# Attention slots of a decoder trunk: short matmuls in one group, projections in one run, value weights' parts made partly earlier

## The chip, the cores and the metric

One core of a Trainium2 chip runs the whole program. Its engines work side by side, each through its own list of instructions in order: TensorE (PE in the profile, with its weight loads as PEld), VectorE (DVE), ScalarE (ACT), GpSimd (POOL) and SyncE (SP), which issues most transfers. The metric is the device time of one execution in microseconds (us). Lower is better.

## The reference

Two layers work on x of 1024 tokens by 1024 channels in float32. The first layer mixes tokens with a gated MLP on half of its columns and with eight heads of dilated attention on the other half, the second with gated linear attention; each is followed by a gated MLP with a causal convolution. The change lies in the first layer's mixer:

```python
def even_mixer(h, w_in, a_ln_g, a_ln_b, a_ws, a_bs, q_g, k_g, w_out):
    z = h @ w_in
    u, v, q, k, vb = jnp.split(z, [...], axis=-1)
    a_out = chunked_gmlp(gelu(u), gelu(v), a_ln_g, a_ln_b, a_ws, a_bs)
    qh, kh = rms_norm(heads(q), q_g), rms_norm(heads(k), k_g)
    vh = heads(vb)
    for window, dilation in ((128, 1), (512, 4), (2048, 16)):
        o_r, l_r = dilated_branch(qh, kh, vh, window, dilation)
        outs.append(o_r); lses.append(l_r)
    wts = softmax(stack(lses), axis=0)
    o = einsum('rbhs,rbhsc->bhsc', wts, stack(outs))
    return concatenate([a_out, b_out], axis=-1) @ w_out
```

`dilated_branch` attends within blocks of 128 tokens (the own block and the one before), after tokens have been gathered by the dilation. Heads have 64 channels.

## The kernel before

Numbers stay float32 in effect: an operand of a large product is split into a high part and the rest (`split`: a cast on ScalarE, a subtraction on VectorE), and a product is a sum over such parts.

`attention` (from line 870 of the profile's numbering) works in 64 slots. The eight heads form four pairs p; each pair has eight near units (the branch of dilation 1, one unit for each of eight blocks n) and then eight far units (the dilated branches together). `order` lists them. TensorE's work in a slot is of two sorts. The short matmuls belong to the attention itself:

- sc: the scores of a unit, two heads, 128 or 256 columns (`score`, line 885), followed by mask and minimum on VectorE and the exponential on ScalarE (both in tile sm)
- pP: the transposes of the exponentials (`turn`, line 911), copied to pT by ScalarE in odd units and by VectorE in even ones
- po: the outputs, pT times values (`output`, line 922), 4 or 8 matmuls of 64 columns
- tk: the transposes of keys (kd, by `ident`) and queries (qs, by `identr`) of a near unit (`Pair.turn`, line 992), read from one bank of PSUM (tag tq) by ScalarE and VectorE into kT and qT
- pm: the gating MLP's matmuls (`mix`, line 807), called out of the list `mixes`

The long matmuls come from the generator `work`: projections of queries, keys and values for the next pair (pj, 384 columns, 24 for a block of 128 tokens), and after the last pair the gating MLP's pv and pu (512 columns). `take(m)` issues the next m of them. A slot takes a share of 12 while a pair is left to be projected (13 in the first eight slots), and 21 after that. TensorE follows the order of these calls, since the matmuls are pinned to program order.

Before the change a slot issues: `parts` for the near unit three slots on (the normalised q and k are split or scaled, on POOL and VectorE), its own sc, half its share, the po of the slot before, tk for two slots on, the other half, and its pP. `weights()` stands once in each half and makes the split parts of one piece of weights for the next pair, out of the list `spread`, on ScalarE and VectorE; pieces with k under 4 are pinned to program order there. Three slots of preparation (the prologue) stand ahead of slot 0: `parts` of units 0 to 2, and from the second on 12 projections and one tk.

Weights' parts lie in pool wp (eight buffers) or, for some, in pool wx (four). Pair 2's first four pieces use wx, the rest of the pairs 1 to 3 uses wp. The value weights wv are split by `load_half` in one go, as soon as pair 3's projection reaches its fifth block and buffers come free.

Of the kernel before, what the change touches and what calls it, by code (L numbers as in the profile page):

```python
# [11 lines left out]
F32R = mybir.dt.float32r  # L12
U8 = mybir.dt.uint8
I32 = mybir.dt.int32
AF = mybir.ActivationFunctionType
# [5 lines left out]
P = 128  # L21
# [3 lines left out]
KD = D // P  # L25
# [3 lines left out]
PAIRS = 4  # L29
# [25 lines left out]
def f32(ap):  # L55
    return ap.bitcast(F32)
# [11 lines left out]
def trunk(ctx: ExitStack, tc: tile.TileContext, a, out):  # L68
    nc = tc.nc
    V, A, G, T, Q = nc.vector, nc.scalar, nc.gpsimd, nc.tensor, nc.sync  # L70
# [3 lines left out]
    wp = ctx.enter_context(tc.tile_pool(name="wp", bufs=NW, reuse_waits="tile"))  # L74
# [17 lines left out]
    g0 = small.tile([P, KD], F32, tag="g0", bufs=1, name="g0")  # L92
# [21 lines left out]
    def split(dst, src, hi=None, lo=None):  # L114

        (hi or A.copy)(dst[0], src)  # L116
        (lo or V.tensor_sub)(dst[1], src, f32(dst[0]))  # L117

    def turned(dst, t):

        raw = t.dtype == F32R
        return T.transpose(dst.bitcast(F32R) if raw else dst, t, identr if raw else ident)

    def scaled(dst, src, gain):

        split(dst, src, lambda o, x: A.activation(o, x, AF.Copy, scale=gain),
              lambda o, x, h: V.scalar_tensor_tensor(o, x, gain, h, op0=ALU.mult, op1=ALU.subtract))

    def load_raw(src, name, cols=D):
        raw = rawp.tile([P, D], F32, tag="raw", name=name)[:, :cols]  # L130
        Q.dma_start(raw, src)
        return raw

    def parts_of(src, name, pool=None, gain=None, **tag):

        w = (pool or wp).tile([P, 2, 512], F32R, **(tag or {"tag": "w"}), name=name)
        parts = [w[:, i, : src.shape[-1]] for i in range(2)]
        if gain is None:
            split(parts, src)
        else:  # L140
            scaled(parts, src, gain)
        return parts

    def load_w(src, name, width=512, n=2, gains=None):

        raw = load_raw(src, name + "r", n * width)
        return [parts_of(raw[:, i * width : i * width + width], f"{name}_{i}",
                         gain=None if gains is None else gains[:, i : i + 1]) for i in range(n)]

    def load_half(src, name, gains=None):  # L150

        return [w for kp in range(4)
                for w in load_w(src[kp], f"{name}{kp}", gains=None if gains is None else gains[:, 2 * kp : 2 * kp + 2])]
# [601 lines left out]
        V.scalar_tensor_tensor(mboth, count, -math.log(2.0), mboth, op0=ALU.mult, op1=ALU.add)  # L755
        yield

    def load_qkv(p, wx, between=None, spread=None):

        def part(k, src, gain):  # L760
            pin = tc.keep_in_program_order if k < 4 else lambda ins: ins
            if p == 2 and k < 4:
                w = wx.tile([P, 2, 384], F32R, tag="wx", name=f"wx{p}{k}")
            else:
                w = wp.tile([P, 2, 512], F32R, tag="w", name=f"wq{p}{k}")
            ws[k] = [w[:, i, : src.shape[-1]] for i in range(2)]
            split(ws[k], src, lambda o, x: pin(A.activation(o, x, AF.Copy, scale=gain)),
                  lambda o, x, h: pin(V.scalar_tensor_tensor(o, x, gain, h, op0=ALU.mult, op1=ALU.subtract)))

        ws = []  # L770
        for kp in range(4):
            raw = load_raw(a["w_qkv"][p, kp], f"wq{p}{kp}r", 768)
            if between:
                between(kp)
            for i in range(2):
                k = 2 * kp + i
                w = (2 * k) % 8 + k // 4 if p == 0 else k
                src, gain = raw[:, i * 384 : i * 384 + 384], g0[:, w : w + 1]
                if spread is not None:
                    ws.append(None)  # L780
                    spread.append(partial(part, k, src, gain))
                elif p % 2 or k >= 4:
                    ws.append(parts_of(src, f"wq{p}{kp}_{i}", gain=gain))
                else:
                    w = wx.tile([P, 2, 384], F32R, tag="wx", name=f"wx{p}{k}")
                    ws.append([w[:, j, :] for j in range(2)])
                    scaled(ws[-1], src, gain)
        return ws
# [49 lines left out]
    def pin(ins):  # L838
        return tc.keep_in_program_order(ins) if pinned else ins
# [31 lines left out]
    def attention(ps, at, av, pq, pq0, par0, wx, wq0, gqk, masks, rest, gm_open):  # L871
# [5 lines left out]
        def by4(t):  # L877

            return t.rearrange("p s (m r) -> p s r m", r=4)
# [51 lines left out]
        class Pair:  # L931
# [56 lines left out]
            def turn(self, n):  # L988
                qs, kd = self.qs[n]
                t = ps.tile([P, 4, P], F32, tag="tq", name=f"tk{self.p}{n}")  # L990
                for s in range(2):
                    pin(T.transpose(t[:, s, :], kd[:, s, :], ident))
                for j in range(2):
                    pin(turned(t[:, 2 + j, :], qs[:, j, :]))
                split([four(self.kT[:, i * 2 : i * 2 + 2], n) for i in range(2)], by4(t[:, :2]))
                qT = pq.tile([P, 2, P], F32R, tag="qT", bufs=3, name=f"qT{self.p}{n}")
                A.copy(qT, t[:, 2:])
                G.tensor_copy(four(self.qR, n), by4(f32(qT)))
                self.qT[n] = qT
# [54 lines left out]
        pairs, mixes, first, spread = [], [], [], []  # L1054
        slot = 0

        def weights():
            if slot and spread:
                spread.pop(0)()

        def soon(half, todo):
            mixes.extend([slot + 3 + k / 2, half, f] for k, f in enumerate(todo))

        def mix(when):
            while mixes and when(mixes[0]):
                mixes.pop(0)[2]()

        def work():
            ws = {0: wq0}
            for p in range(PAIRS):  # L1070
                def ahead():
                    ws[p + 1] = load_qkv(p + 1, wx, spread=spread) if p + 1 < PAIRS else load_half(a["w_vu"][0], "wv", g0)
                pairs.append(Pair(p, ws[p]))
                yield from pairs[p].project(ahead)
            par0.close()
            gm = gm_open()
            yield from gmlp(ps, gm, ws[PAIRS], soon)
            yield from u_proj(ps, gm, load_half(a["w_vu"][1], "wu", g0), lambda half: mix(lambda m: m[1] <= half), first)
# [3 lines left out]
        def take(m):  # L1082
            for _ in range(m):
                ins = next(stream, None)
                if ins is not None:
                    if pairs[0].done > 1:
                        tc.keep_in_program_order(ins)

        def need(p, n):
            while len(pairs) <= p or pairs[p].done <= n:  # L1090
                take(1)
# [12 lines left out]
        def turns(i):  # L1104
            p, kind, n = place_of(i)
            if kind == "n":
                pairs[p].turn(n)

        pinned.append(True)
        for i in range(3):  # L1110
            need(0, i + 2)
            parts(i)
            if i:
                take(12)
                turns(i - 1)
        need(0, BEGUN)
        previous = None
        for slot, (p, kind, n) in enumerate(order):
            share = RATE[0] if slot < NT else RATE[1] if len(pairs) < PAIRS or pairs[-1].done < NT else RATE[2]
            parts(slot + 3)  # L1120
            score, turn, output = pairs[p].near_unit(n) if kind == "n" else pairs[p].far_unit(n)
            score()
            weights()
            take(share // 2)
            if previous:
                previous()
            turns(slot + 2)
            mix(lambda m: m[0] <= slot)
            weights()
            take(share - share // 2)  # L1130
            mix(lambda m: m[0] <= slot + 0.5)
            turn()
            previous = output
            if kind == "n" and p and n in (4, 6):
                combine(pairs[p - 1], n // 2 - 2)()
        take(6)
        previous()
        for k, ins in enumerate(stream):
            pin(ins)
            if k % 12 == 11 and mixes:  # L1140
# [403 lines left out]
    def gm_open():  # L1544
        return gms.enter_context(tc.tile_pool(name="gm", bufs=1, side="right", reuse_waits="tile"))
# [13 lines left out]
    for l in range(2):  # L1559
        w_out = a["od_w_out" if l else "ev_w_out"]  # L1560
        x_in = (lambda n: x2[n]) if l else (lambda n: rows(a["x"], n))
        with ExitStack() as ops:
# [3 lines left out]
            pool = ops.enter_context(tc.tile_pool(name=f"op{l}", bufs=2, side="right", reuse_waits="tile"))  # L1566
# [41 lines left out]
        with ExitStack() as st:  # L1608
            pool = st.enter_context(tc.tile_pool(name=f"fd{l}", bufs=1, reuse_waits="tile"))
# [112 lines left out]
```

## Time and profile before

| | |
|---|---|
| median of 3 runs | 2118.29 us (2117.88 to 2118.57) |
| profiled execution | 2118.6 us |
| its span | 2116.9 us |
| granted clock of TensorE | 1.000 |
| TensorE busy | 2105.9 us, 99% |
| VectorE, ScalarE, POOL busy | 1536.3, 1055.7, 475.2 us |
| the attention stage | about 5.8 to 357 us of the span |

Times in rows of the timeline are from the span's start. A row gives start, duration, engine, line of the kernel, operation, tile written and tiles read, shapes and count; a bracket names the idle time ahead of it and what ended that. Tiles carry no numbers there: pT3n is any transposed tile of pair 3's near units. TensorE's matmuls are pipelined and their ends are modelled, so neighbouring rows overlap.

### The profile page before, as it was taken

The numbers are of one execution on the slowest core, as the hardware profiler recorded it, in microseconds if no ns is written. First come the engines' busy times: TensorE is split into PE (matmuls) and PEld (weight loads), VectorE is DVE, ScalarE is ACT, GpSimd is POOL, SyncE is SP. The second block draws the span as 40 slices with busy tenths as digits, with TensorE's granted clock in tenths as the row PEclk, the third lists the DMA queues.
The fourth block names the chain that finished last, engine by engine and source line by source line (L and its number), as shares of the span: only waits on it lengthen the run. The fifth ranks groups of instructions, "written<-read, shape, count | busy, mean of one in ns | idle before, by whom it ended". The sixth has DMA issues, their size and how long they took to land. (4 is left out here: it accounts for less than half of the span.)

```text
span 2116.9 us, 29739 instructions
## 1 busy us (share of the span) xinstructions
PE 2105.9 (99%) x10440; PEld 1794.1 (85%) x10440; DVE 1536.3 (73%) x2486; ACT 1055.7 (50%) x2061; POOL 475.2 (22%) x479
## 2 busy tenths in 40 slices
PE   8999999999999999999999999999999999999999
PEld 8999888888888888888899888888888888888887
DVE  7566564677879888655578777886788788785554
ACT  7556563365444444444454466745544444444443
POOL 5334310014325344000010011101224344220000
PEclk9999999999999999999999999999999999999999
DMA  7222314854444444765554243596544544458564
GB/s 250 59 75 65 101 50 156 306 199 157 165 144 159 169 164 150 263 229 203 207 191 156 87 137 134 169 328 239 196 162 155 169 164 154 155 179 299 204 227 160
DMA packets 170278, 367.08 MB, mean 173 GB/s; under 512 B 17632, under 2 KB 61408, under 8 KB 170128
## 3 DMA queue, kind: packets, MB, share of 16 engines
q1 hardware_dynamic: 169984, 365.05, 50.5%
q8 instruction: 82, 1.34, 0.3%
q14 instruction: 68, 0.56, 0.1%
q10 hardware_dynamic: 144, 0.13, 0.0%
HBM read 248.39 MB, written 115.93 MB: 172 GB/s over the span
## 5 line engine op out<-in xcount | busy, mean ns | idle before, releaser
L117 DVE TENSOR_TENSOR da<-ar,da 128x512 fp32r<-128x512 f32 x154 | 106.2, 690 | 155.1 <-ACT da L116 155.1
L116 ACT CAST da<-ar 128x512 fp32r<-128x512 f32 x154 | 96.0, 623 | 214.2 <-PE pdQ L427 101.6
L218 PE MATMUL po<-wo,hq 128*128 128x512 f32 x768 | 183.1, 394 | 0.0
L218 PEld LDWEIGHTS po<-wo,hq 128*128 128x128 f32 x768 | 142.1, 188 | 28.5 <-DVE hq L117 0.3
L218 PE MATMUL pv<-wv,hq 128*128 128x512 f32 (+2 forms) x768 | 142.2, 340 | 0.0
L427 PE MATMUL pdC<-dw,da 128*128 128x512 f32 x528 | 134.8, 390 | 0.0
L427 PE MATMUL pdB<-dw,da 128*128 128x512 f32 x528 | 134.8, 390 | 0.0
L218 PEld LDWEIGHTS pv<-wv,hq 128*128 128x128 f32 x768 | 118.7, 189 | 14.2
L218 PE MATMUL pj<-wq,hq 128*128 128x384 f32 x576 | 121.0, 343 | 0.0
L427 PEld LDWEIGHTS pdC<-dw,da 128*128 128x128 f32 x528 | 99.1, 188 | 20.5
L427 PEld LDWEIGHTS pdB<-dw,da 128*128 128x128 f32 x528 | 98.8, 188 | 20.3
L286 POOL TENSOR_TENSOR S1g<-rg 128x512 f32<-128x512 f32 x20 | 29.7, 1485 | 378.5 <-DMA wsd<-D 300.7
L117 DVE TENSOR_TENSOR dw<-wr,dw 128x512 fp32r<-128x512 f32 x154 | 105.6, 686 | 8.0 <-ACT dw L116 7.6
L161 POOL TENSOR_SCALAR rn<-ssq 128x1 f32<-128x1 f32 x22 | 9.1, 416 | 431.6 <-ACT h L181 242.5
L427 PE MATMUL pdO<-dw,da 128*128 128x512 f32 x396 | 100.5, 389 | 0.0
L116 ACT CAST dw<-wr 128x512 fp32r<-128x512 f32 x154 | 95.0, 617 | 6.6 <-DMA wr<-in_w_dn 2.9
L218 PEld LDWEIGHTS pj<-wq,hq 128*128 128x128 f32 x576 | 97.0, 189 | 0.0
L427 PEld LDWEIGHTS pdO<-dw,da 128*128 128x128 f32 x396 | 74.3, 188 | 15.4
L351 DVE SCALAR_TENSOR_TENSOR t<-g,cw,t 128x1022 f32<-128x1022 f32 x44 | 74.8, 1700 | 0.1
L335 DVE TENSOR_TENSOR g<-g,s1g 128x512 f32<-128x512 f32 x22 | 16.3, 741 | 78.7 <-ACT s1g L334 78.7
L350 DVE SCALAR_TENSOR_TENSOR t<-g,cw,t 128x1023 f32<-128x1023 f32 x44 | 59.4, 1350 | 14.8 <-ACT t L349 14.8
L161 POOL TENSOR_SCALAR ro<-oss 128x1 f32<-128x1 f32 x32 | 9.4, 294 | 255.5 <-ACT og L1437 255.5
(1052 smaller groups left out, 5480.8 us busy)
## 6 DMA issues: line engine op xcount, KB each, us to landing
ar<-actd SPq DMA_DIRECT2D x70, 512.0 KB, 3.6
rd<-in_w_down SPq DMA_DIRECT2D x44, 512.0 KB, 3.7
wsd<-D SPq DMA_DIRECT2D x88, 256.0 KB, 2.4
rg<-in_w_gate SPq DMA_DIRECT2D x40, 512.0 KB, 3.6
ru<-in_w_up SPq DMA_DIRECT2D x40, 512.0 KB, 4.9
wr<-wsd SPq DMA_DIRECT2D x40, 512.0 KB, 4.3
actd<-t SPq DMA_DIRECT2D x66, 256.0 KB, 2.2
wr<-in_w_dn SPq DMA_DIRECT2D x30, 512.0 KB, 5.0
```

What stands on the lines that cost most here:

```text
L116: (hi or A.copy)(dst[0], src)
L117: (lo or V.tensor_sub)(dst[1], src, f32(dst[0]))
L161: eng.tensor_scalar(r, ssq, 1.0 / n, EPS, op0=ALU.mult, op1=ALU.add)
L218: yield T.matmul(o, L[i], R[jj][:, sl], start=(k == 0 and (ii, jj) == PASSES[0]), stop=(k == nk - 1 and (ii, jj) == PASSES[-1]))
L286: G.tensor_tensor(sums[name], x, y, op=op)
L335: V.tensor_add(C22, C22, s1)
L350: V.scalar_tensor_tensor(t[:, 1:], g[:, : S - 1], w(1), t[:, 1:], op0=ALU.mult, op1=ALU.add)
L351: V.scalar_tensor_tensor(t[:, 2:], g[:, : S - 2], w(0), t[:, 2:], op0=ALU.mult, op1=ALU.add)
L427: T.matmul(o, L[ii][:, t * P : t * P + P], R[jj], skip_group_check=more, start=start and not more and (ii, jj) == PASSES[0], stop=stop and ...
```

## The change

A slot now issues, in this order: the po of the unit two slots back, the pP of the unit one slot back, its own sc, tk for two slots on, any pm that is due, one piece of weights, half the share, another piece, and the rest of the share. The two halves follow each other without anything for TensorE between them, so all short matmuls of a slot form one group and its projections one run. Outputs come one slot later. In the prologue 6 projections instead of 12 precede a tk. After the last slot come an output, the last pP, 9 long matmuls and the last output. Pieces of the gating (`soon`) are due two slots later for the second half of the tokens, and one instead of half a slot apart.

The spread part of `load_qkv` becomes `load_spread`, and the value weights go through it too: their pieces are put on the list when pair 3's projection reaches its fifth block, and are made two to a slot. Pair 3's last four pieces now lie in wx, so four buffers of wp are free for wv's first four as soon as pair 2's pieces there have been used.

```diff
--- before.py
+++ after.py
@@ -755,17 +755,25 @@
         V.scalar_tensor_tensor(mboth, count, -math.log(2.0), mboth, op0=ALU.mult, op1=ALU.add)
         yield
 
-    def load_qkv(p, wx, between=None, spread=None):
-
-        def part(k, src, gain):
+    def load_spread(src, name, width, gains, spread, pool):
+
+        def part(k, raw):
             pin = tc.keep_in_program_order if k < 4 else lambda ins: ins
-            if p == 2 and k < 4:
-                w = wx.tile([P, 2, 384], F32R, tag="wx", name=f"wx{p}{k}")
-            else:
-                w = wp.tile([P, 2, 512], F32R, tag="w", name=f"wq{p}{k}")
-            ws[k] = [w[:, i, : src.shape[-1]] for i in range(2)]
-            split(ws[k], src, lambda o, x: pin(A.activation(o, x, AF.Copy, scale=gain)),
+            own = pool(k)
+            w = own.tile([P, 2, 384], F32R, tag="wx", name=f"{name}{k}") if own else \
+                wp.tile([P, 2, 512], F32R, tag="w", name=f"{name}{k}")
+            ws[k] = [w[:, i, :width] for i in range(2)]
+            gain = gains[:, k : k + 1]
+            split(ws[k], raw, lambda o, x: pin(A.activation(o, x, AF.Copy, scale=gain)),
                   lambda o, x, h: pin(V.scalar_tensor_tensor(o, x, gain, h, op0=ALU.mult, op1=ALU.subtract)))
+
+        ws = [None] * KD
+        for kp in range(4):
+            raw = load_raw(src[kp], f"{name}{kp}r", 2 * width)
+            spread += [partial(part, 2 * kp + i, raw[:, i * width : i * width + width]) for i in range(2)]
+        return ws
+
+    def load_qkv(p, wx, between=None):
 
         ws = []
         for kp in range(4):
@@ -776,10 +784,7 @@
                 k = 2 * kp + i
                 w = (2 * k) % 8 + k // 4 if p == 0 else k
                 src, gain = raw[:, i * 384 : i * 384 + 384], g0[:, w : w + 1]
-                if spread is not None:
-                    ws.append(None)
-                    spread.append(partial(part, k, src, gain))
-                elif p % 2 or k >= 4:
+                if k >= 4:
                     ws.append(parts_of(src, f"wq{p}{kp}_{i}", gain=gain))
                 else:
                     w = wx.tile([P, 2, 384], F32R, tag="wx", name=f"wx{p}{k}")
@@ -1054,12 +1059,15 @@
         pairs, mixes, first, spread = [], [], [], []
         slot = 0
 
+        def wx_of(p):
+            return lambda k: wx if (p, k // 4) in ((2, 0), (3, 1)) else None
+
         def weights():
             if slot and spread:
                 spread.pop(0)()
 
         def soon(half, todo):
-            mixes.extend([slot + 3 + k / 2, half, f] for k, f in enumerate(todo))
+            mixes.extend([slot + 3 + 2 * half + k, half, f] for k, f in enumerate(todo))
 
         def mix(when):
             while mixes and when(mixes[0]):
@@ -1069,7 +1077,8 @@
             ws = {0: wq0}
             for p in range(PAIRS):
                 def ahead():
-                    ws[p + 1] = load_qkv(p + 1, wx, spread=spread) if p + 1 < PAIRS else load_half(a["w_vu"][0], "wv", g0)
+                    ws[p + 1] = load_spread(a["w_qkv"][p + 1], f"wq{p + 1}", 384, g0, spread, wx_of(p + 1)) if p + 1 < PAIRS else \
+                        load_spread(a["w_vu"][0], "wv", 512, g0, spread, wx_of(PAIRS))
                 pairs.append(Pair(p, ws[p]))
                 yield from pairs[p].project(ahead)
             par0.close()
@@ -1111,30 +1120,32 @@
             need(0, i + 2)
             parts(i)
             if i:
-                take(12)
+                take(6)
                 turns(i - 1)
         need(0, BEGUN)
-        previous = None
+        ended, scored = [], []
         for slot, (p, kind, n) in enumerate(order):
             share = RATE[0] if slot < NT else RATE[1] if len(pairs) < PAIRS or pairs[-1].done < NT else RATE[2]
             parts(slot + 3)
             score, turn, output = pairs[p].near_unit(n) if kind == "n" else pairs[p].far_unit(n)
+            for f in ended:
+                f()
+            for f, _ in scored:
+                f()
             score()
-            weights()
-            take(share // 2)
-            if previous:
-                previous()
             turns(slot + 2)
             mix(lambda m: m[0] <= slot)
             weights()
+            take(share // 2)
+            weights()
             take(share - share // 2)
-            mix(lambda m: m[0] <= slot + 0.5)
-            turn()
-            previous = output
+            ended, scored = [f for _, f in scored], [(turn, output)]
             if kind == "n" and p and n in (4, 6):
                 combine(pairs[p - 1], n // 2 - 2)()
-        take(6)
-        previous()
+        ended[0]()
+        scored[0][0]()
+        take(9)
+        scored[0][1]()
         for k, ins in enumerate(stream):
             pin(ins)
             if k % 12 == 11 and mixes:
```

TensorE in a near slot of pair 0 (sc0n40 and sc0n41 are the scores of unit 4 for its two heads, tk06 the transposes of unit 6, pT0n3 and pT0n2 the transposed exponentials of units 3 and 2). Before:

```order
L885 MATMUL sc0n40_991<-kT0_454,qT04_889 128x256 x2
L885 MATMUL sc0n41_997<-kT0_454,qT04_889 128x256 x2
L218 MATMUL pj10_972<-wq11_823,hq10_92 128x384
L218 MATMUL pj10_972<-wq12_869,hq00_90 128x384 x3
L218 MATMUL pj10_972<-wq13_892,hq10_92 128x384 x2
L922 MATMUL po0n0_810<-vN02_564,pT0n3_983 128x64
L922 MATMUL po0n0_810<-vN03_609,pT0n3_983 128x64
L922 MATMUL po0n0_810<-vN02_564,pT0n3_983 128x64
L922 MATMUL po0n0_810<-vN03_609,pT0n3_983 128x64
L992 MATMUL tk06_1017<-ident_78,kd06_912 128x128 x2
L122 MATMUL tk06_1017<-identr_83,qs06_909 128x128 x2
```

After:

```order
L927 MATMUL po0n0_847<-vN01_524,pT0n2_912 128x64
L927 MATMUL po0n0_847<-vN02_564,pT0n2_912 128x64
L927 MATMUL po0n0_847<-vN01_524,pT0n2_912 128x64
L927 MATMUL po0n0_847<-vN02_564,pT0n2_912 128x64
L916 MATMUL pP0n3_983<-ident_78,sm0n30_917 128x128 x2
L916 MATMUL pP0n3_983<-ident_78,sm0n31_923 128x128 x2
L890 MATMUL sc0n40_991<-kT0_454,qT04_876 128x256 x2
L890 MATMUL sc0n41_997<-kT0_454,qT04_876 128x256 x2
L997 MATMUL tk06_1003<-ident_78,kd06_901 128x128 x2
L122 MATMUL tk06_1003<-identr_83,qs06_898 128x128 x2
L218 MATMUL pj10_968<-wq11_820,hq10_92 128x384
L218 MATMUL pj10_968<-wq12_879,hq00_90 128x384 x3
```

The outputs are now unit 2's instead of unit 3's and stand ahead of the scores, pP of unit 3 has joined them, tk06 stands right behind the scores, and the six projections that parted scores and outputs are gone from there.

ScalarE around the value weights (sm are exponentials, wv0_0 to wv3_1 before and wv0 to wv7 after the eight pieces' high parts). Before:

```order
L959 ACTIVATE qn36_3344<-pj36_3239,r0_89 128x256
L961 ACTIVATE vN36_3346<-pj36_3239,r0_89 128x128
L891 ACTIVATE sm3n11_3338,ot3n0_3273<-sm3n11_3338,ot3n0_3273 128x256
L126 ACTIVATE wv0_0_3023<-wv0r_3021,g0_88 128x512
L116 CAST kT3_2623<-tk33_3362 128x8x32
L126 ACTIVATE wv0_1_3026<-wv0r_3021,g0_88 128x512
L126 ACTIVATE wv1_0_3031<-wv1r_3029,g0_88 128x512
L913 COPY pT3n1_3383<-pP3n1_3378 128x512
L126 ACTIVATE wv1_1_3034<-wv1r_3029,g0_88 128x512
L997 CAST qT33_3369<-tk33_3362 128x256
L891 ACTIVATE sm3n20_3393,ot3n0_3273<-sm3n20_3393,ot3n0_3273 128x256
L126 ACTIVATE wv2_0_3039<-wv2r_3037,g0_88 128x512
```

After:

```order
L964 ACTIVATE qn36_3354<-pj36_3249,r0_89 128x256
L966 ACTIVATE vN36_3356<-pj36_3249,r0_89 128x128
L1002 CAST qT33_3348<-tk33_3341 128x256
L767 ACTIVATE wv4_3132<-wv2r_3025,g0_88 128x512
L767 ACTIVATE wv5_3178<-wv2r_3025,g0_88 128x512
L767 ACTIVATE wv6_3187<-wv3r_3027,g0_88 128x512
L918 COPY pT3n1_3388<-pP3n1_3383 128x512
L116 CAST kT3_2633<-tk34_3402 128x8x32
L896 ACTIVATE sm3n20_3393,ot3n0_3273<-sm3n20_3393,ot3n0_3273 128x256
L767 ACTIVATE wv7_3232<-wv3r_3027,g0_88 128x512
L896 ACTIVATE sm3n21_3399,ot3n0_3273<-sm3n21_3399,ot3n0_3273 128x256
L1002 CAST qT34_3409<-tk34_3402 128x256
```

Four of the eight pieces (wv0 to wv3) have left this stretch for an earlier one, and wv4 to wv6 stand in a row ahead of the copy of pT3n1, which before had three pieces ahead of it and five behind it.

TensorE in the prologue, at the transposes of unit 1. Before:

```order
L218 MATMUL pj05_685<-wx00_341,hq01_91 128x384 x3
L218 MATMUL pj05_685<-wx01_344,hq01_91 128x384 x3
L218 MATMUL pj05_685<-wx02_356,hq01_91 128x384 x3
L218 MATMUL pj05_685<-wx03_359,hq01_91 128x384 x3
L218 MATMUL pj05_685<-wq02_0_367,hq11_93 128x384
L992 MATMUL tk01_704<-ident_78,kd01_635 128x128 x2
L122 MATMUL tk01_704<-identr_83,qs01_632 128x128 x2
L218 MATMUL pj05_685<-wq02_0_367,hq11_93 128x384 x2
```

After:

```order
L218 MATMUL pj05_685<-wx00_341,hq01_91 128x384 x3
L218 MATMUL pj05_685<-wx01_344,hq01_91 128x384 x3
L218 MATMUL pj05_685<-wx02_356,hq01_91 128x384
L997 MATMUL tk01_698<-ident_78,kd01_635 128x128 x2
L122 MATMUL tk01_698<-identr_83,qs01_632 128x128 x2
L218 MATMUL pj05_685<-wx02_356,hq01_91 128x384 x2
L218 MATMUL pj05_685<-wx03_359,hq01_91 128x384 x3
```

tk01 now stands six projections earlier in block 5.

## The prediction, made before the changed kernel ran

> **What bounds the kernel now.** I read the page first, for the engine that is busiest.
>
> ```profile
> span 2116.9 us, 29739 instructions
> PE 2105.9 (99%) x10440; PEld 1794.1 (85%) x10440; DVE 1536.3 (73%) x2486; ACT 1055.7 (50%) x2061; POOL 475.2 (22%) x479
> ```
>
> TensorE (PE) is busy 2105.9 of 2116.9 us. It leaves 11.0 us in all, so only TensorE's own time or one of its few waits can be won. The change touches only the attention of the first layer, so the next view is the busy time by stretch of it (columns: stretch, its length, busy time and count of PE, PEld, DVE, ACT and POOL, the granted clock, DMA share, GB/s).
>
> ```profile
> 36.00:100.00 64.00, 63.43 (x452) 61.82 (x451) 38.27 (x125) 42.23 (x128) 26.40 (x45) 1.00 0.22 64
> 100.00:232.00 132.00, 131.96 (x958) 130.24 (x957) 82.40 (x270) 78.44 (x248) 56.47 (x93) 1.00 0.28 77
> 232.00:240.00 8.00, 7.17 (x51) 6.29 (x50) 8.00 (x20) 7.57 (x20) 3.15 (x4) 1.00 0.61 179
> 240.00:357.00 117.00, 117.00 (x614) 99.22 (x613) 67.29 (x176) 60.60 (x118) 19.13 (x27) 1.00 0.27 84
> ```
>
> The clock is 1.00 throughout. TensorE waits in two places only: 0.57 us just after 36, and 0.83 us at 232 to 240, where VectorE is busy 8.00 of 8.00 us and ScalarE 7.57. Everywhere else its time is the sum of its matmuls, and the change issues the same matmuls. So the question is what a matmul costs in another neighbourhood, and what becomes of two small waits.
>
> **Grouping.** A near slot before alternates: weights' transposes and scores (pP, sc), six projections (pj), outputs and key transposes (po, tk), six projections. The timeline of TensorE (start, duration, both in us):
>
> ```profile
> 110.51 0.60 PE L911 MATMUL pP1n<-ident,sm1n 128*128 128x128 f32 x4
> 110.86 0.72 PE L885 MATMUL sc1n<-kT,qT 128*128 128x256 f32 x4
> 111.42 0.69 PE L218 MATMUL pj<-wq,hq 128*128 128x384 f32 x3
> 111.95 0.70 PE L218 MATMUL pj<-wx,hq 128*128 128x384 f32 x3
> 112.48 1.00 PE L922 MATMUL po1n<-vN,pT1n 128*128 128x64 f32 x8
> 113.32 0.39 PE L992 MATMUL tk<-ident,kd 128*128 128x128 f32 x2
> ...
> 113.67 1.28 PE L218 MATMUL pj<-wx,hq 128*128 128x384 f32 x6
> 114.79 0.60 PE L911 MATMUL pP1n<-ident,sm1n 128*128 128x128 f32 x4
> ```
>
> Durations overlap, so I price a group by starts: from its first row to the next group's first row, less the long matmuls between. The long matmul's price comes from an undisturbed run, and the same stretch shows the transposes alone:
>
> ```profile
> 25.31 2.24 PE L218 MATMUL pj<-wx,hq 128*128 128x384 f32 x12
> 27.39 0.34 PE L218 MATMUL pj<-wq,hq 128*128 128x384 f32 x1
> 27.57 0.38 PE L992 MATMUL tk<-ident,kd 128*128 128x128 f32 x2
> ...
> 27.91 2.15 PE L218 MATMUL pj<-wq,hq 128*128 128x384 f32 x11
> 29.89 0.33 PE L218 MATMUL pj<-wx,hq 128*128 128x384 f32 x1
> ```
>
> Twelve pj take 27.39 − 25.31 = 2.08 us, 0.173 each. Then pP and sc cost 112.48 − 110.51 − 6 × 0.173 = 0.93 us, po x8 with tk costs 114.79 − 112.48 − 1.04 = 1.27, and tk alone costs 29.89 − 27.57 − 11 × 0.173 = 0.41. The outputs alone stand in the far slots:
>
> ```profile
> 271.61 1.00 PE L922 MATMUL po3n<-vN,pT3n 128*128 128x64 f32 x8
> 272.42 2.79 PE L218 MATMUL pv<-wv,hq 128*128 128x512 f32 x11
> 275.05 0.38 PE L911 MATMUL pP3d<-ident,sm3d 128*128 128x128 f32 x2
> ...
> 275.74 2.46 PE L218 MATMUL pv<-wv,hq 128*128 128x512 f32 x10
> 278.04 0.56 PE L922 MATMUL po3d<-v,pT3d 128*128 128x64 f32 x4
> 278.41 2.79 PE L218 MATMUL pv<-wv,hq 128*128 128x512 f32 x11
> 281.03 0.60 PE L911 MATMUL pP3d<-ident,sm3d 128*128 128x128 f32 x4
> ```
>
> A pv takes (278.04 − 275.74) / 10 = 0.230, so po x8 alone costs 275.05 − 271.61 − 2.53 = 0.91 us, and po x4 costs 281.03 − 278.04 − 2.53 = 0.46. Two things follow. Half the matmuls cost half the time, so a group has no fixed price for its switch from and to long ones. And po with tk costs 1.27 where the two apart cost 0.91 + 0.41 = 1.32: transposes behind outputs save 0.05 us.
>
> After the change one group holds po, pP, sc and, in near slots, tk. Two joints are new and stand nowhere in the trace: po then pP (64 slots, less the first ones without an output), and sc then tk (29 slots that have both an output and a transpose; three of the 32 transposes are in the prologue). The transposes in pP go by ident like the first half of tk, so po then pP is nearest to po then tk and I take −0.05; its other end is 0. For sc then tk I take tk at its price alone, which gives the old saving back: +0.05, with −0.05 beside it at the other end had tk kept its saving there and sc shared too. In near slots the two cancel; in the 32 others 32 × −0.05 = **−1.6 us**. The ends are −1.6 − 29 × 0.05 = −3.1, all joints saving, and 29 × 0.05 = +1.5, none saving and tk's old saving gone.
>
> On this the Trainium skill speaks against the change: "TensorE: Matmul & The Clock Gate", section "Step-by-step: what each phase is for", says that the next weight load is pulled ahead and runs while the current matmul streams. By that, a short matmul right behind a long one has its load hidden, and a merged group has half as many such places. The trace does not agree for these groups: 0.46 is half of 0.91, so no first load is free.
>
> **Value weights.** Before, eight ScalarE casts and eight VectorE subtractions for wv come at once; now four of the pairs are made before pair 3's last units, four behind them. The wait and its cause:
>
> ```profile
> 230.45 0.86 PE L911 MATMUL pP3n<-ident,sm3n 128*128 128x128 f32 x4
> ...
> 231.62 1.21 PE L218 MATMUL pj<-wq,hq 128*128 128x384 f32 x6
> 233.45 1.10 PE L922 MATMUL po3n<-vN,pT3n 128*128 128x64 f32 x8 [0.62 <-ACT pT3n L913]
> ...
> 236.79 0.69 PE L218 MATMUL pj<-wq,hq 128*128 128x384 f32 x3
> 237.31 0.86 PE L218 MATMUL pv<-wv,hq 128*128 128x512 f32 x3
> 238.38 1.10 PE L922 MATMUL po3n<-vN,pT3n 128*128 128x64 f32 x8 [0.21 <-DVE pT3n L913]
> 230.73 0.71 ACT L126 ACTIVATE wv<-wv0r,g 128x512 fp32r<-128x512 f32 x1
> ...
> 232.84 0.56 ACT L913 COPY pT3n<-pP3n 128x512 f32<-128x512 f32 x1
> ...
> 238.09 0.72 ACT L126 ACTIVATE wv<-wv3r,g 128x512 fp32r<-128x512 f32 x1
> ```
>
> The first of eight casts starts at 230.73, the last at 238.09, and the copy of the transposed weights (pT3n) queues among them. TensorE loses 233.45 − 231.62 − 1.06 (the same six pj before an unhindered po, 111.42 to 112.48) = 0.77; 238.38 − 236.79 − 3 × 0.173 − 3 × 0.230 = 0.38; and 0.86 − 0.60 = 0.26 in the first pP. That is 1.41 us. In the new order four casts (4 × 0.72 = 2.9 us) remain there, three in a row ahead of one pT copy, but the copy's outputs now come a whole slot later, 4.28 us (113.32 less 4.28 is where the tk before it starts). The exponentials behind those casts are what is late next: casts 2.9, copy 0.56 and two exponentials of about 0.5 nearly fill the 4.28 us, and I leave 0.15 us for that. The term is **−1.3 us**, from 0 (the exponentials take the place of the copies) to −1.4. The four parts made early go to stretches where ScalarE is busy 78.44 of 132 us and VectorE 82.40; the buffers they need are freed with pair 2's last projections. Loads of the raw weights keep their queue and order.
>
> The gating's pieces (mx and pm) start up to 3.5 slots later, the combination of a pair's two branches stands ahead of the next copies on VectorE, and the last pair's outputs come one slot later. The instructions are the same, and what hides them is the room on VectorE and ScalarE in 240 to 357 us, 67.29 and 60.60 busy of 117. I take 0 for these together and carry their upper end in the small waits below: if that cover is gone, a pm or a pT waits as po does now, 0.2 to 0.6 us once. POOL's splits of q and k (qs, kd) are issued one slot ahead of tk as before, and tk stands half a run, about 1.0 us, nearer to them; POOL is busy 56.47 of 132 us, so this is 0 as well.
>
> **Prologue.** Six projections instead of twelve precede each early tk, so tk for units 0 and 1 comes 1.04 us earlier, and tk for unit 2 right behind unit 0's scores. There is one bank for tk, and it is read late; the second line is a statistics pass that ScalarE does ahead of the next unit's exponentials, the third the wait that is there now.
>
> ```profile
> 31.75 0.38 ACT L997 CAST qT<-tk 128x256 fp32r<-128x256 f32 x1 [0.49 <-DVE kT L117]
> 37.86 1.04 ACT L671 ACTIVATE xq<-xq 128x1024 f32<-128x1024 f32 x1
> 44.93 1.10 PE L922 MATMUL po0n<-vN,pT0n 128*128 128x64 f32 x8 [0.48 <-ACT pT0n L913]
> ```
>
> The present waits for pT0n (0.57 us by the window, with what durations hide about 1.0) go, since outputs come a slot later. In their place I expect tk for unit 1 to wait about 0.65 us for the bank's last reader at 31.75 and the first pP about as long for the exponential behind the 1.04 us pass. The term is **0**, from −0.9 (nothing new) to +0.8 (both, with a second tk late).
>
> **Sum.** −1.6 − 1.3 + 0 = −2.9 us; I add +0.2 for small new waits (between 0 and 0.5, the size of the present ones), which gives −2.7. The profiled execution took 2118.6 us, 1.7 above its span and 0.3 above the median of 2118.29. So 2115.9 for such an execution, 2115.6 against the median. About 0.2% (4.24 us) is what a measurement of this kernel can tell from no change: the bounds are 2114.05 and 2122.53.
>
> **The rivals.** First, grouping buys nothing: the joints cost 0 on balance, and only the weights' term counts. 2118.29 − 1.3 = 2117.0. For it speaks that half a group costs half; against it, the 0.05 between po and tk.
>
> Second, everything gains: −3.1 − 1.4 − 0.9 = −5.4, 2112.9. It needs sc then tk to share as po then tk does, and a prologue without any new wait.
>
> Third, slower: the single tk bank. Its reads go ScalarE, VectorE, ScalarE, and weight parts queue among them:
>
> ```profile
> 109.42 1.61 DVE L768 SCALAR_TENSOR_TENSOR wq<-wq23r,g,wq 128x384 fp32r<-128x384 f32 x2
> 111.46 0.37 ACT L997 CAST qT<-tk 128x256 fp32r<-128x256 f32 x1 [1.38 <-DVE kT L117]
> ```
>
> The tk of 109.04 is read to the end at 111.83, 2.8 us on, since VectorE does 1.61 us of wq first. The next one comes at 4.28 us, so 1.5 us is left; the two parts per slot now stand elsewhere in the queues. If they delay each read by more than that, every excess 0.1 us costs 2.4 us over the 24 near slots of pairs 0 to 2. It decides from 0.3 us on: 24 × 0.3 = 7.2, less 2.7, gives 2122.8. Against it speaks the 1.5 us of room, nearly one whole slot's weight work.
>
> Fourth, slower too: the merged group loses one hidden weight load a slot. A po costs 0.91 / 8 = 0.11, so 61 joints × 0.11 = +6.7, with −1.3 for the weights 2123.7. The halves of po speak against it. The page named above stands behind this one; by that rule it would come so, by the trace not.
>
> **How the numbers follow.** My sum, with its terms between their ends, 0.44; grouping without effect 0.22; everything gains 0.20; the bank 0.07; the lost load 0.05; small waits that eat the gain, within 0.2%, 0.02. That makes faster 0.20, same 0.68, slower 0.12. I predict 2115.7 us. The range reaches from 2113.2, near the case where everything gains, to 2119.8, where no joint saves (+1.5) and the weights' wait stays: it leaves out both slow rivals and a little of the fast end.
>
> **What would show it.** In the timeline: near slots of 4.28 us or less; a far group of po x8, pP x2 and sc at 1.55 instead of 0.91 + 0.69 = 1.60 (0.69 is 278.04 − 275.05 − 2.30); TensorE's idle time at 230 to 240 under 0.3 us instead of 0.83; a wait of about 0.65 us before the second tk at 30 to 32. Wrong would be waits on qT, kT or the exponentials inside near slots, or near slots over 4.35 us.

## The result and the profile after

The changed kernel took 2114.57 us (median, 2114.19 to 2115.71), the kernel before, run beside it, 2118.36 us. The ratio is 0.9982, 95% interval 0.9975 to 0.9989: 3.8 us faster, between 2.3 and 5.3. The profiled execution took 2114.53 us with a span of 2112.8, against 2118.6 and 2116.9 before. Two more timings of the changed kernel, taken as a base for the experiments, gave 0.9985 and 0.9981. The median of before moved between 2118.3 and 2119.0 from chip to chip, so each kernel is compared by its ratio to before on the same chip.

The page, then the busy time of the same four stretches (stretch, length, busy time and count of PE, PEld, DVE, ACT, POOL, clock, DMA share, GB/s), then TensorE's waits in the attention:

```profile
span 2112.8 us, 29740 instructions
PE 2102.1 (99%) x10440; PEld 1793.6 (85%) x10440; DVE 1533.2 (73%) x2486; ACT 1058.7 (50%) x2063; POOL 471.3 (22%) x479
36.00:100.00 64.00, 63.58 (x459) 62.87 (x458) 38.52 (x123) 42.02 (x129) 26.56 (x46) 1.00 0.22 64
100.00:232.00 132.00, 131.95 (x966) 131.54 (x964) 84.39 (x281) 82.97 (x255) 56.41 (x91) 1.00 0.27 78
232.00:240.00 8.00, 8.00 (x58) 7.39 (x57) 6.39 (x18) 4.81 (x17) 4.88 (x8) 1.00 0.94 277
240.00:357.00 117.00, 117.00 (x616) 99.83 (x615) 62.85 (x166) 62.13 (x115) 14.87 (x23) 1.00 0.23 74
...
PE pP0n L916 <- ACT sm0n L896: 0.4, 1, 0.4
PE tk L997 <- ACT qT L1002: 0.3, 1, 0.3
```

TensorE is busy 3.8 us less with the same 10440 matmuls. That is not all matmuls that cost less: their ends are modelled, so short waits are hidden inside busy time, and the sums below separate the two. The stretch of the value weights has no idle time left, 8.00 of 8.00, with ScalarE down from 7.57 to 4.81. Two waits are still listed, both early: tk for the reader of its bank, and a pP for an exponential.

The timeline of TensorE after, one near slot and two far ones of pair 3, to be held against 110.51 to 114.79 and 271.61 to 281.03 before:

```profile
117.06 1.00 PE L927 MATMUL po1n<-vN,pT1n 128*128 128x64 f32 x8
117.90 0.61 PE L916 MATMUL pP1n<-ident,sm1n 128*128 128x128 f32 x4
118.26 0.72 PE L890 MATMUL sc1n<-kT,qT 128*128 128x256 f32 x4
118.82 0.38 PE L997 MATMUL tk<-ident,kd 128*128 128x128 f32 x2
...
119.16 2.34 PE L218 MATMUL pj<-wq,hq 128*128 128x384 f32 x12
121.34 1.00 PE L927 MATMUL po1n<-vN,pT1n 128*128 128x64 f32 x8
...
270.15 1.00 PE L927 MATMUL po3n<-vN,pT3n 128*128 128x64 f32 x8
...
276.49 0.56 PE L927 MATMUL po3d<-v,pT3d 128*128 128x64 f32 x4
...
282.57 1.00 PE L927 MATMUL po3d<-v,pT3d 128*128 128x64 f32 x8
```

A near slot takes 121.34 − 117.06 = 4.28 us, as before. Two far slots of pair 3 take 282.57 − 270.15 = 12.42 us. Before it was 12.63, by these two rows of the old trace:

```profile
271.61 1.00 PE L922 MATMUL po3n<-vN,pT3n 128*128 128x64 f32 x8
284.24 1.00 PE L922 MATMUL po3d<-v,pT3d 128*128 128x64 f32 x8
```

So a far slot among pv saves 0.10 us. Far slots among pj, before and after, with two slots between the rows:

```profile
133.14 1.00 PE L922 MATMUL po1n<-vN,pT1n 128*128 128x64 f32 x8
140.28 1.00 PE L922 MATMUL po1d<-v,pT1d 128*128 128x64 f32 x8
```

```profile
132.89 1.00 PE L927 MATMUL po1n<-vN,pT1n 128*128 128x64 f32 x8
139.89 1.00 PE L927 MATMUL po1d<-v,pT1d 128*128 128x64 f32 x8
```

7.14 us became 7.00, 0.07 a slot. Pairs 0 to 2 have 24 slots without tk and the last pair has ten. If each saves what these few do, 0.07 and 0.10, grouping gives 1.7 + 1.0 = 2.7 us, an estimate. The value weights' waits, 1.41 us by the prediction's rows, are gone. Idle time in the early waits went from 0.57 to 0.67 us (0.25 at the second tk, 0.42 between 36 and 100). Together −2.7 − 1.4 + 0.1 = −4.0, against 4.1 between the two spans and 3.8 between the medians.

The starts of single matmuls give a second account, in which waits that the modelled ends hide are seen too. From the 25th projection to the end of the stage the two traces differ by 4.2 us. About 1.9 of it stands at the joints of the groups (34 slots without tk at 0.05 each give 1.7), 0.8 inside the runs, and 1.5 in waits. The waits at the value weights, 1.65 us by this count, are gone. The early ones go from 1.5 to 1.3 us, and those of pP for exponentials in far slots grow from 0.2 to 0.6. Outside this stretch the two traces differ by −0.3 us ahead of it and by +0.4 behind it. No run shows the cause of these two.

### The profile page after: what moved, and what is told of

The parts are those of the page before. It is cut to its first block, busy times and chain, and to the rows that moved or that the text cites. A ratio compares the mean times of both kernels' runs of the same rounds, so it can differ in the third digit from the quotient of the medians.

```text
span 2112.8 us, 29740 instructions
## 1 busy us (share of the span) xinstructions
PE 2102.1 (99%) x10440; PEld 1793.6 (85%) x10440; DVE 1533.2 (73%) x2486; ACT 1058.7 (50%) x2063; POOL 471.3 (22%) x479
## 5 line engine op out<-in xcount | busy, mean ns | idle before, releaser
L218 PE MATMUL pj<-wq,hq 128*128 128x384 f32 x672 | 128.6, 339 | 0.0
L218 PEld LDWEIGHTS pj<-wq,hq 128*128 128x128 f32 x672 | 114.8, 188 | 0.0
```

What stands on the lines that cost most here:

```text
L218: yield T.matmul(o, L[i], R[jj][:, sl], start=(k == 0 and (ii, jj) == PASSES[0]), stop=(k == nk - 1 and (ii, jj) == PASSES[-1]))
```

## The experiments

Where the text gives a group's price to the nanosecond, it is counted from the starts of the single matmuls in the trace, from the last long one ahead of the group to the second one behind it, less the two long ones.

**The value weights alone** (slot order, prologue and gating of before):

```diff
-ws[p + 1] = load_qkv(p + 1, wx, spread=spread) if p + 1 < PAIRS else load_half(a["w_vu"][0], "wv", g0)
+ws[p + 1] = load_spread(..., spread, wx_of(p + 1)) if p + 1 < PAIRS else load_spread(..., spread, wx_of(PAIRS))
```

> The slot order and prologue of before, with only the value weights' part of the change: their pieces two to a slot, four of them ahead of pair 3's end, pair 3's last four pieces in the other pool. Theory A (fewer casts in one place remove the wait): the three TensorE waits at 230 to 240 us, 1.65 us together in the trace of before, go almost wholly, 2118.4 - 1.5 = 2116.9 us. Theory B (what removed them is that outputs come a slot later): at least one po of pair 3 still waits 0.3 to 0.8 us for its pT behind the remaining casts, and the time is 2117.4 to 2118.2 us. Groups and their prices stay as before in both.

Ratio 0.9994 (0.9986 to 1.0003), −1.3 us. The medians alone do not tell this from no change; the timeline does, in which one po still comes late:

```profile
231.07 1.22 PE L218 MATMUL pj<-wq,hq 128*128 128x384 f32 x6
232.32 1.10 PE L927 MATMUL po3n<-vN,pT3n 128*128 128x64 f32 x8
```

It starts 1.25 us after the run instead of 1.06, where before it was 1.83, and the other two waits are gone. Fewer casts in the place are enough for most of it. What is left goes with the outputs' old place half a slot behind pP: the changed kernel, which differs here in the slot's order, has no such wait.

**The grouping alone** (value weights split at once, pair 3's pieces in the old pool):

```diff
-load_spread(a["w_vu"][0], "wv", 512, g0, spread, wx_of(PAIRS))
+load_half(a["w_vu"][0], "wv", g0)
-... in ((2, 0), (3, 1)) else None
+... in ((2, 0),) else None
```

> The changed slot order and prologue, but the value weights split in one go as before and pair 3's pieces in the old pool. Theory A (grouping saves about 2.0 us at the joints and 0.8 us in the long runs, the waits for weights are another matter): some wait at the value weights comes back, now in pP for the exponentials, 0.5 to 1.6 us, and the time is 2115.0 to 2116.3 us. Theory B (later outputs hide the casts): no TensorE wait over 0.3 us there, and the time is that of the changed kernel, 2114.6 us.

Ratio 0.9988 (0.9980 to 0.9997), −2.5 us. The two halves of the change add up to the whole, −1.3 and −2.5 against −3.8, each known to about 1.8 us either way. A wait came back, but not where either theory had it:

```profile
233.71 0.72 PE L890 MATMUL sc3n<-kT,qT 128*128 128x256 f32 x4
235.42 0.41 PE L997 MATMUL tk<-ident,kd 128*128 128x128 f32 x2 [0.99 <-ACT qT L1002]
...
233.07 1.34 ACT L126 ACTIVATE wv<-wv2r,g 128x512 fp32r<-128x512 f32 x2
234.29 0.73 ACT L126 ACTIVATE wv<-wv3r,g 128x512 fp32r<-128x512 f32 x1
234.90 0.37 ACT L1002 CAST qT<-tk 128x256 fp32r<-128x256 f32 x1
```

The read of the one tk bank (qT) stands on ScalarE behind three casts of wv, and the next tk waits for it. Later outputs do take pT out of the way of the casts; the bank is then what is late.

**Scores last in the group, tk ahead of pP:**

```diff
 for f in ended: f()
+turns(slot + 2)
 for f, _ in scored: f()
 score()
-turns(slot + 2)
```

> The changed kernel with tk moved inside the group, from behind the scores to between outputs and pP. Theory C (a joint from outputs to transposes saves 0.04 to 0.05 us, and what the long run pays is set by the group's last short matmul: after tk or po it pays, after sc it does not): near groups of 2.172 us fall to about 2.12, 29 x 0.05 = -1.5 us, 2113.1 us. Theory D (each group saves one joint whatever stands last): near groups stay at 2.17 us and the time at 2114.6 us. A loss would be pP waiting longer for nothing here, since tk stands ahead of it, or sc for its kT.

Ratio 0.9992 (0.9983 to 1.0001). The near slots did get cheaper:

```profile
113.43 1.00 PE L927 MATMUL po1n<-vN,pT1n 128*128 128x64 f32 x8
114.27 0.39 PE L997 MATMUL tk<-ident,kd 128*128 128x128 f32 x2
...
117.64 1.00 PE L927 MATMUL po1n<-vN,pT1n 128*128 128x64 f32 x8
```

4.21 us instead of 4.28; the group costs 2.119 instead of 2.172, the 0.05 expected. The kernel is slower than the changed one all the same, by 2.1 us, so waits took this back and more:

```profile
PE tk L997 <- POOL kd L988: 0.6, 1, 0.6
PE tk L997 <- issue: 0.5, 1, 0.5
PE tk L997 <- ACT qT L1002: 0.5, 1, 0.5
```

**Outputs apart again**, alone between the two halves of the run:

```diff
-for f in ended: f()
 for f, _ in scored: f()
 score(); turns(slot + 2); mix(...); weights(); take(share // 2)
+for f in ended: f()
 weights(); take(share - share // 2)
```

> The changed kernel with the outputs taken out of the group and put between the two halves of the run, alone there. Theory C (the joint from outputs to pP is what saves): every slot loses it, 61 x 0.05 = +3.0 us, and the six matmuls behind each break run some ns slower, +0.8, so 2118.4 us. Theory D (only the number of runs counts, the joint itself saves nothing): +0.8 us at most, 2115.4 us.

Ratio 1.0008 (0.9999 to 1.0017), 5.5 us over the changed kernel's 0.9982, and no better than before though the value weights' part is in it. Near slots:

```profile
112.86 1.00 PE L927 MATMUL po1n<-vN,pT1n 128*128 128x64 f32 x8
...
117.18 1.00 PE L927 MATMUL po1n<-vN,pT1n 128*128 128x64 f32 x8
```

4.32 us. By single starts the group of pP, sc and tk costs 1.332 and po alone 0.895, 2.227 together against 2.172 in one group; in far slots 0.701 + 0.895 = 1.596 against 1.543. So the joint from outputs to pP is worth 0.05 us a slot. The joints are not the whole of the loss. By single starts the trace loses 4.7 us in the stage against the changed kernel's: about 2.8 at the joints, 1.1 inside the runs, and 0.9 in waits, which neither theory had. At the joints merging is not a gain by itself; what follows the outputs is.

**A prologue of 12 projections** (`take(12)` for `take(6)`):

> The changed kernel with 12 projections instead of 6 ahead of each early tk. Theory A (the second tk waits for the last reader of the one tk bank because it comes 1.04 us earlier): that wait of 0.45 us falls to 0.15 us or less, but the waits of pP for exponentials in the first units stay: 0.1 to 0.4 us faster than the changed kernel. Theory B (the wait only moves, because slot 0 comes at the same place): no difference over 0.1 us, the wait standing at a later tk or pP.

Ratio 0.9987, against 0.9985 for the changed kernel timed beside it: no difference. The wait moved one tk on:

```profile
31.73 0.38 PE L997 MATMUL tk<-ident,kd 128*128 128x128 f32 x2
...
35.86 0.41 PE L997 MATMUL tk<-ident,kd 128*128 128x128 f32 x2 [1.06 <-ACT qT L1002]
```

The changed kernel itself, as base of this and the next two:

> The changed kernel itself, on the same chip as the next three, as their base: 3.8 us under before, as in its first runs. The waits in its prologue (0.45, 0.27 and 0.58 us) may differ a little with the arrival of the first weights.

**tk apart**, between the halves:

```diff
 score()
-turns(slot + 2)
 mix(...); weights(); take(share // 2)
+turns(slot + 2)
 weights(); take(share - share // 2)
```

> The changed kernel with tk taken out of the group and put between the two halves of the run. Theory C (the price of a group is set by what stands last in it): the group's rest then ends on sc at 1.76 us and tk alone costs 0.41, together the 2.17 us of now, so near slots lose nothing at the joints and only the run's matmuls behind each break run slower, +0.3 to +0.5 us in all. Theory D (each further break costs one joint of 0.05 us): 29 x 0.05 = +1.5 us more, +1.9 us in all.

Ratio 0.9991 (0.9982 to 1.0000) against 0.9985; the difference lies within the intervals. The groups are unambiguous: 1.759 without tk and 0.414 for tk alone, 2.173 against 2.172. Breaking the run costs nothing at the joint from scores to tk. In its trace three tk lost 0.24, 0.24 and 0.56 us to waits.

**tk and scores exchanged:**

```diff
 for f, _ in scored: f()
-score()
 turns(slot + 2)
+score()
```

> The changed kernel with tk and sc exchanged: outputs, pP, tk, scores. tk stands 0.55 us earlier than in the changed kernel and 0.35 us later than in the run with tk ahead of pP, where it waited 1.6 us in all for kd and the bank. Theory C: near groups with scores last cost 2.12 us instead of 2.17, 29 x 0.05 = -1.5 us; if tk's waits stay under 0.3 us in all, 1.2 to 1.5 us faster than the changed kernel. Theory E (the 0.55 us eats the room of kd and of the bank): waits of 0.5 to 1.5 us at tk come, and the time is that of the changed kernel within 0.5 us.

Ratio 0.9994 (0.9985 to 1.0003). The group costs 2.176 us: nothing won, though the scores stand last. That refutes the form in which I had put the rule. The starts show where the price goes. The first wide matmul behind tk holds up the one behind it, whether they are projections (0.245 us from start to start instead of 0.174) or scores (0.187 instead of 0.120). A transpose behind tk or po pays 0.02 us or less. Scores behind pP pay nothing: the last transpose of pP takes 0.08 us less there and the first scores 0.08 more. So the saving is where outputs or tk are followed by transposes, and that scores stand last does not matter.

**tk one slot ahead**, in the order outputs, tk, pP, scores:

```diff
 for f in ended: f()
+turns(slot + 1)
 for f, _ in scored: f()
 score()
-turns(slot + 2)
```

> The order outputs, tk, pP, scores again, but with tk only one slot ahead of its scores instead of two, and one tk less in the prologue, so that kd has been ready for a slot longer when tk comes. Theory F (what saves is outputs or tk followed by transposes, 0.05 each time, and the run with tk ahead of pP lost its gain to tk's waits for kd and the bank, 1.6 us): near groups cost 2.12 us as in that run, the waits for kd vanish, and the time is 1.0 to 2.0 us under the changed kernel. Theory G (kT and qT now come too late for the next slot's scores, 2.8 us after tk, or tk still waits for the bank): waits at sc or tk of 0.05 us and more in many of the 29 near slots, and the time is that of the changed kernel or up to 5 us more.

Ratio 0.9994 (0.9985 to 1.0003), beside 0.9981 for the changed kernel, the base here:

> The changed kernel once more, as the base of the run beside it on the same chip: 3.0 to 3.8 us under before.

The groups cost 2.119 to 2.122 as in the other run of that order and the waits for kd went, but tk waits longer:

```profile
PE tk L997 <- issue: 2.7, 3, 1.1
...
234.45 0.37 ACT L1002 CAST qT<-tk 128x256 fp32r<-128x256 f32 x1 [0.77 <-DVE kT L117]
234.92 0.41 PE L997 MATMUL tk<-ident,kd 128*128 128x128 f32 x2 [1.11 <-issue]
```

The profile names no releaser, but tk starts 0.10 us after the bank's last reader (qT, 234.45 + 0.37) has ended, here and at 38.01, where qT ends at 37.91. I read it as the bank, which these two times suggest and no run shows by itself.

**Two banks for tk**, paid for by one bank for both heads' scores, with tk one and two slots ahead:

```diff
-("sc", 2), ("pj", 2), ("po", 1), ("tq", 1)
+("sc", 1), ("pj", 2), ("po", 1), ("tq", 2)
-sc = ps.tile([P, 256], F32, tag="sc", ...)
+sc = ps.tile([P, 2, 256], F32, tag="sc", ...)
```

> The run with tk one slot ahead, and two PSUM banks for tk instead of one; the scores of a unit's two heads share one bank for that, so the mask waits for both heads' scores. Theory F (in the run with one bank tk waited for the bank's last reader only): the 2.7 us of waits at tk vanish, near groups stay at 2.12 us, and the time is 1.0 to 2.0 us under the changed kernel's 3.6 us under before, that is 2113.0 to 2114.0 us at a before of 2118.6. Theory G (the readers are late whatever the bank, and their lateness moves to the scores, which need kT and qT in the next slot): waits of the same size at sc, and no gain over the run with one bank, 2117.4 us.

> Outputs, tk, pP, scores with tk two slots ahead of its scores, as in the run with scores last, and two banks for tk, one for the scores of both heads. Theory F: of that run's waits the 1.0 us for the bank go, the 0.6 us for kd stay, near groups cost 2.12 us, and the time is 0.5 to 1.2 us under the changed kernel. Theory G: no gain over the run with scores last, since each exponential now starts later behind the pair of scores and pP waits for it, 0.05 us or more in many slots.

Both took 1.0364 times before (1.0350 to 1.0378), 77 us more. Neither theory was tested: in one tile the second head's scores wait until VectorE has masked the first head's. Over the whole stage the first of the two runs lists such a wait in all 64 units, 64 us of idle time together. The rest of the 77 was not followed up; by single starts the long matmuls inside the runs take about 5 us more, beside a granted clock of 0.96 from 100 to 232 us, where the changed kernel has 1.00.

```profile
113.66 0.42 PE L889 MATMUL sc1n<-kT,qT 128*128 128x128 f32 x2
114.75 0.44 PE L889 MATMUL sc1n<-kT,qT 128*128 128x128 f32 x2 [0.67 <-DVE ot1n L894]
...
PE sc1n L889 <- DVE ot1n L894: 11.1, 8, 2.3
PE sc2n L889 <- DVE ot2n L894: 9.5, 8, 2.3
```

Whether a second bank would let the cheaper order win stays open. Of the kernels run, none was faster than the changed one.

## Why the prediction was right, and where its sizes were off

I forecast 2115.7 us, −2.7, a change too small to be told; it measured −3.8. That is inside the bound of 4.24 by a small margin, the interval reaches to 5.3, and with 18 runs of each kernel it can be told from none. The mechanisms came, and the choice for each new joint was right. Nearly all of the difference is the grouping term.

- **Grouping, −1.6 forecast, −2.7 measured.** The joints came as taken. Outputs then pP save 0.05 us (0.053 in far slots, by the run with outputs apart); scores then tk is tk at its price alone (0.413), so near slots stay at 4.28. The term was too small because I priced long matmuls as fixed. A far slot among pj saves 0.07 and not 0.05, among pv 0.10: behind a short group the first matmuls of a run are a few ns slower, and one run in place of two has that once. By starts inside the runs, outside the groups, this is 0.8 us in all. I had also miscounted: 28 slots have both an output and a tk, since two of the early tk stand in the prologue and two in the first two slots, which have no output, and 34 slots have outputs without tk. The case "everything gains" did not come: the near joints did not save.
- **The lost weight load** did not come either. What I wrote beside it, that no first load is free, was too simple. By single starts the second matmul of po follows 0.055 us after the first, the others 0.111. In the trace with tk one slot ahead, where po follows a run as in the changed kernel, the first weight load of po starts 0.18 us before its matmul, while the projections still run (PEld is the weight load):

```profile
231.25 1.72 PE L218 MATMUL pj<-wq,hq 128*128 128x384 f32 x9
...
232.64 1.03 PEld L927 LDWEIGHTS po3n<-vN,pT3n 128*128 128x128 f32 x8
232.82 1.00 PE L927 MATMUL po3n<-vN,pT3n 128*128 128x64 f32 x8
```

  This agrees with the Trainium skill ("TensorE: Matmul & The Clock Gate", "Step-by-step: what each phase is for"), which says that the next weights load while the current matmul runs. The long matmul behind po then pays about 0.06 us. The two cancel in a group alone, which is why half a group cost half and the prediction saw nothing hidden. Followed by transposes, po keeps the first and sheds the second. That is the joint's 0.05. That the load is what the 0.055 and the 0.06 come from is argued from these times; no run changes it alone.
- **Value weights, −1.3 forecast, −1.4 measured** (−1.65 by single starts). The wait vanished. I named the exponentials as what is late next; when the casts were put back it was the bank of tk.
- **Prologue, 0 forecast, +0.1 measured in idle time.** The second tk waited for the bank's last reader as forecast, with 0.25 us of idle time for the 0.65 expected, and 0.45 and 0.69 us in the two further traces of the changed kernel. The wait moves along when the tk's place is changed. The pP wait came too, 0.28 us by single starts for the exponential behind the statistics pass. A larger one, 0.36 us of idle time, stands three slots further on, where the second exponential follows a piece of weights on ScalarE:

```profile
30.72 0.40 ACT L1002 CAST qT<-tk 128x256 fp32r<-128x256 f32 x1
31.26 0.41 PE L997 MATMUL tk<-ident,kd 128*128 128x128 f32 x2 [0.25 <-ACT qT L1002]
...
50.44 0.61 ACT L767 ACTIVATE wq<-wq13r,g 128x384 fp32r<-128x384 f32 x1
50.95 0.50 ACT L896 ACTIVATE sm0n<-sm0n,ot0n 128x256 f32<-128x256 f32 x1
51.59 0.44 PE L916 MATMUL pP0n<-ident,sm0n 128*128 128x128 f32 x2 [0.36 <-ACT sm0n L896]
```

  Both are waits for an exponential inside a near slot, which the prediction named as a sign of being wrong. They come only in pair 0, and by single starts all the early waits together are no longer than before. The +0.2 for small new waits stands against +0.4 at pP in far slots.
- **The bank as rival** did not decide for this order, whose near slots show no tk wait. It came up in the runs that moved tk inside the slot or put the casts back, also where tk stood later, between the halves.

## What to carry to other kernels

Where TensorE is the bound, price a short matmul by what follows it: outputs and tk followed by a projection, and tk followed by scores, paid 0.05 to 0.07 us here, followed by transposes 0.02 or less, while pP followed by scores paid nothing. A better order is worth that times its count, and only if the operands of what moves forward and the buffer it writes are ready. Here the order that saved up to 1.5 us at the joints ran 2.1 to 2.7 us slower in all, because of waits. Before a shared buffer is split among more users, look at what else waits on the tile as a whole.

## What I had not expected

- A run of long matmuls does not have one price: by single starts, pv are 0.224 to 0.236 us apart in the first eight or so behind a group (0.230 on average at the second to fourth) and 0.226 to 0.227 from the twelfth on. With runs of twice the length the stage gained 0.8 us.
- Which transposes stand in the joint matters: pP then tk saved nothing (2.176 us), tk then pP saved 0.05 (2.119).
- Two heads' scores in one tile made TensorE wait about 1 us a unit, 64 of the 77 us that these runs lost.
